# A row maximum on one core: 16 loads in place of 17, 56 blocks for GpSimd in place of 36, and results turned back four at a time

## The chip, the cores and the metric

The kernel runs on one core of one Trainium2 chip. The metric is the device time of one execution in microseconds (us); lower is better. A core has five engines that run side by side, each on its own queue of instructions: TensorE (PE), VectorE (DVE), ScalarE (ACT), GpSimd (POOL) and SyncE (SP). Transfers between the chip's main memory (HBM) and the core's on-chip memory (SBUF) run on 16 DMA engines; here SP issues the loads and ACT the stores. PSUM is the small memory that TensorE writes.

## The reference

The input is 64 MB of 4-byte numbers, and the output is the maximum of each row of 1024.

```python
def setup_inputs():
    batch, seq, dim = 32, 512, 1024
    return {"x": np.random.randn(batch, seq, dim).astype(np.float32)}

def reference(x):
    return np.max(x, axis=-1).astype(np.float32)
```

## The kernel before

The 16384 rows lie over 128 partitions, 128 rows to each. "A load of n rows" below means n rows of 1024 numbers on each partition, in one transfer. `BLOCKS` lists the loads in order: twelve of 2, 16, 14, 15, 13, 12, 10, 9, 8, 7, 6 and 4 rows, then five of 3, 2, 2, 1 and 1. The last 3 rows come in six column pieces, `PIECES`, of 640 to 384 columns, two pieces to a row; the second piece of a row has the first one's result in the cell ahead of it, so that its reduce covers both.

Loads land in a ring of `RING` = 47 rows. `issue` (L273) sends a load as soon as the program has named the last reader of the rows that it overwrites; SP then waits for these readers, and for an earlier transfer with the same semaphore, of which there are eight. The pieces (L278) follow the loads on the same queue.

`PLAN` is the order of all work, written out by hand; `in_turn` ties each engine to it. A step is a letter and a number:

- `d` and `p` are VectorE's reduces of load j (L76). `d` takes whole rows into the result tile `res`, and `p` takes the columns that VectorE keeps of the rows that it shares with GpSimd. `f` reduces a piece.
- `t`, `c`, `r`, `b`, `e` are GpSimd's share, by chunks of up to eight blocks of 128 columns. TensorE turns each 128x128 block into PSUM (`turn`, L155), so that a row of the input lies across the partitions. ACT copies the chunk to SBUF (`fetch`, L166). GpSimd takes the maximum over the partitions (`across`, L173), and all partitions then hold the results. TensorE turns them back from one row to a column, block by block (`back`, L184), and ACT copies the small columns out of PSUM (`keep`, L194).
- `m` is VectorE's merge of these with its own part: `m10` for load 10 and `m99` for all the last loads together, whose parts lie in `joint`.

`SHARED` says for each load how many rows are shared, how many blocks of each row go to GpSimd, and how many rows make a chunk:

```python
SHARED = {10: (6, 3, 2, 0), 12: (3, 3, 2, 0), 14: (2, 3, 1, 0), 16: (1, 3, 2, 0)}
```

That is 18 + 9 + 6 + 3 = 36 blocks in eight chunks. The functions `select` and `sums` stand in the code, and no step of the plan names them. Two stores end the kernel, both issued by ACT: the first behind the first piece's reduce (L313), the second behind everything on VectorE (L321).

Of the kernel before, what the change touches and what calls it, by code (L numbers as in the profile page):

```python
# [8 lines left out]
F32 = mybir.dt.float32  # L9
# [1 line left out]


BLOCKS = [
    [2, 16, 14, 15, 13, 12, 10, 9, 8, 7, 6, 4],
    [3, 2, 2, 1, 1],
]
RING = 47

SHARED = {10: (6, 3, 2, 0), 12: (3, 3, 2, 0), 14: (2, 3, 1, 0), 16: (1, 3, 2, 0)}


RANK = {12: 1, 14: 2, 16: 2}


PIECES = [(2, 640), (1, 512), (0, 576), (1, 512), (0, 448), (2, 384)]


PLAN = """  # L30
    d0 d1 d2 d3 d4 d5 d6 d7 d8 d9 t0 p10 t1 c0 r0 t2 c1 d11 r1 c2 b0 e0 r2 b1 e1 t3 p12 t4
    c3 b2 c4 r3 d13 e2 r4 m10 t5 p14 b3 c5 t6 r5 d15 e3 b4 c6 t7 p16 e4 r6 b5 f0 c7 e5 f1 r7
    b6 f2 e6 f3 b7 f4 e7 f5 m99
""".split()

NOSYNC = mybir.DependencyInfo(mybir.DependencyClass.NoSync, mybir.DependencyReason.DATA)
# [4 lines left out]
def kernel(  # L41
# [5 lines left out]
    nc = tc.nc  # L47
    P = 128
    X = mybir.AxisListType.X
    ALU = mybir.AluOpType  # L50

    xf = x.flatten_outer_dims()
    N, D = xf.shape
# [2 lines left out]
    of = out.flatten_outer_dims()  # L56

    once = ctx.enter_context(tc.tile_pool(name="once", bufs=1))
    turned = ctx.enter_context(tc.tile_pool(name="turned", bufs=2))
    allr = ctx.enter_context(tc.tile_pool(name="allr", bufs=2))  # L60
    psum = ctx.enter_context(tc.tile_pool(name="psum", bufs=2, space=bass.MemoryType.PSUM))
    psmall = ctx.enter_context(tc.tile_pool(name="psmall", bufs=4, space=bass.MemoryType.PSUM))

    ring = once.tile([P, I + RING * D], F32)
    res = ring[:, :I]
# [3 lines left out]
    def in_turn(engine, inst):  # L69
        if engine in latest:  # L70
            tc.add_manual_dep(inst.ins, latest[engine].ins.name, NOSYNC, reason="in turn")
        latest[engine] = inst
        return inst

    def maximum(out, in_):
        return in_turn("DVE", nc.vector.reduce_max(out=out, in_=in_, axis=X))  # L76

    ident = once.tile([P, P], F32)
    colno = once.tile([P, P], F32)
    rowno = once.tile([P, 32], F32)  # L80
    in_turn("DVE", nc.vector.memset(ident, 1.0))  # L81
    in_turn("DVE", nc.vector.memset(rowno, 0.0))
# [1 line left out]
        out=colno, data0=ident, data1=ident, initial=-1.0, op0=ALU.add, op1=ALU.mult))  # L84
    in_turn("DVE", nc.vector.transpose(out=rowno, in_=colno[:, :32]))  # L85
    for q in range(1, P // 32):
        part = rowno[q * 32:(q + 1) * 32, 0:1]
        in_turn("DVE", nc.vector.tensor_scalar(  # L88
            out=part, in0=part, scalar1=float(q * 32), scalar2=None, op0=ALU.add))
    in_turn("DVE", nc.vector.tensor_scalar(  # L90
        out=ident, in0=colno, scalar1=rowno[:, 0:1], scalar2=None, op0=ALU.is_equal))

    loads = []
    views = []
    last = 1 + max(r for r, _ in PIECES)
    first = at = 0
    for sizes in BLOCKS:
# [5 lines left out]
        base = len(loads)  # L103
        b, place = 0, {}
        for i in sorted(range(len(sizes)), key=lambda i: RANK.get(base + i, 0)):
            place[i] = b
            b += sizes[i]
        for i, n in enumerate(sizes):
            if at + n > RING:
                at = 0  # L110
            b = place[i]
# [3 lines left out]
    assert first == I  # L115
    shared = [SHARED.get(j, (0, C, 1, 0)) for j in range(len(loads))]

    lead = [n - s[0] for (_, n, _, _), s in zip(loads, shared)]
    final = [j for j in range(len(loads)) if j in RANK]
    final.sort(key=lambda j: loads[j][3])  # L120
# [2 lines left out]
    count = sum(shared[j][0] for j in final)  # L123
    width = max(shared[j][1] + (shared[j][1] < C) for j in final)
    joint = once.tile([P, count, width], F32)

    chunks = []
    for j, (m, parts, per, _) in enumerate(shared):
# [2 lines left out]
    def rows(j):  # L131
        start, n, _, _ = loads[j]
        return ring[:, I + start * D:I + (start + n) * D].rearrange("p (i d) -> p i d", d=D)

    filled, turns, tops = {}, {}, {}
    fetched = {}
    smalls = {}

    def share(j):
        m, parts, _, _ = shared[j]  # L140
        if j in RANK:
            r = loads[j][3] + lead[j] - col0
            return joint[:, r:r + m, :]
        if j not in fetched:
            fetched[j] = once.tile([P, m, parts + (parts < C)], F32, name=f"parts{j}")
        return fetched[j]

    def turn(k):
        j, r, q = chunks[k]
        parts = shared[j][1]  # L150
        ps = psum.tile([P, D], F32)
        for i in range(q):
            for c in range(parts):
                w = (i * parts + c) * P
                in_turn("PE", nc.tensor.transpose(  # L155
                    out=ps[:, w:w + P],
                    in_=rows(j)[:, lead[j] + r + i, c * P:(c + 1) * P],
                    identity=ident,
                ))
        filled[k] = ps  # L160

    def fetch(k):
        j, _, q = chunks[k]
        W = q * shared[j][1] * P
        sb = turned.tile([P, D], F32)
        in_turn("ACT", nc.scalar.copy(out=sb[:, :W], in_=filled[k][:, :W]))  # L166
        turns[k] = sb

    def across(k):
        j, _, q = chunks[k]  # L170
        W = q * shared[j][1] * P
        top = allr.tile([P, D], F32)
        in_turn("POOL", nc.gpsimd.partition_all_reduce(  # L173
            top[:, :W], turns[k][:, :W], P, bass_isa.ReduceOp.max))
        tops[k] = top

    def back(k):
        j, r, q = chunks[k]
        parts = shared[j][1]
        small = psmall.tile([P, q, parts], F32)  # L180
        for i in range(q):
            for c in range(parts):
                w = (i * parts + c) * P
                in_turn("PE", nc.tensor.transpose(  # L184
                    out=small[:, i, c:c + 1],
                    in_=tops[k][0:1, w:w + P],
                    identity=ident[0:1, 0:1],
                ))

        smalls[k] = small  # L190
# [2 lines left out]
        j, r, q = chunks[k]  # L193
        in_turn("ACT", nc.scalar.copy(out=share(j)[:, r:r + q, :shared[j][1]], in_=smalls[k]))  # L194

    def select(k):
        j, _, q = chunks[k]
        B = q * shared[j][1]
        view = tops[k][:, :B * P].rearrange("p (b w) -> p b w", w=P)
        in_turn("POOL", nc.gpsimd.affine_select(  # L200
            out=view, in_=view, pattern=[[0, B], [-1, P]], compare_op=ALU.is_equal,
            fill=0.0, base=0, channel_multiplier=1))

    def sums(k):
        j, r, q = chunks[k]
        parts = shared[j][1]
        for i in range(q):
            for c in range(parts):
                w = (i * parts + c) * P
                in_turn("ACT", nc.scalar.activation(  # L210
                    out=tops[k][:, w:w + P], in_=tops[k][:, w:w + P],
                    func=mybir.ActivationFunctionType.Copy,
                    accum_out=share(j)[:, r + i, c:c + 1]))

    def direct(j):
        _, n, _, col = loads[j]
# [4 lines left out]
    def partial(j):  # L221
        m, parts = shared[j][:2]

        s = width - parts if j in RANK else 1
        maximum(share(j)[:, :, parts:], rows(j)[:, lead[j]:lead[j] + m, parts * P:].rearrange(
# [15 lines left out]
    chained = {}  # L241
    for r, w in PIECES:
        c, q = done[r], before[r]
# [12 lines left out]
    readers = [0] * len(loads)  # L256
# [6 lines left out]
    behind = None  # L263
# [17 lines left out]
    taken = {}  # L281
    settled = -1
    gate = once.tile([P, 2], F32)
    steps = {"t": turn, "c": fetch, "r": across, "b": back, "e": keep, "s": select, "x": sums, "m": merge}
    for step in PLAN:
        issue()
        kind, k = step[0], int(step[1:])
# [8 lines left out]
        elif kind == "f":  # L296
            q = chained.get(k)
# [4 lines left out]
            inst = taken[k] = maximum(*tail[k])  # L302
            if q is not None:
                tc.declare_no_dep(inst.ins, taken[q].ins, reason="the wait stands ahead of it")
            if behind is None:
                behind = inst
# [44 lines left out]
```

## Time and profile before

| what | value |
|---|---|
| median of 3 runs | 163.49 us (163.42 to 163.67) |
| the profiled execution | 163.5 us |
| its span in the profile | 161.7 us |
| VectorE busy | 135.5 us (84%), 33 instructions |
| GpSimd busy | 15.9 us (10%), 8 all-reduces |
| PE, ACT busy | 13.2 us, 7.3 us |
| HBM read | 67.11 MB, mean 415 GB/s over the span |

The span runs from the first instruction to the last that the profiler saw; the execution's time has 1.8 us around it. In the page's slices the span is cut into 40 equal parts, and each digit is the busy share of a part in tenths. A group's row gives the line, the engine and the operation, output from input with their shapes, the count, the busy time in us, the mean ns of one, and the idle time before it with what ended it. In the timeline, rows that follow each other are merged, with their count behind an x. In the chain of work that ended last, "issue" is time in which the engine waited for nothing that the profile shows, and SPq and DVEq are the sequencers of these engines.

### The profile page before, as it was taken

How to read it: one execution, taken by the hardware profiler on the slowest of the kernel's cores; microseconds unless marked ns; L12 is line 12 of the kernel's file. 1: busy time of each engine (PE TensorE's matmuls, PEld its weight loads, DVE VectorE, ACT ScalarE, POOL GpSimd, SP SyncE). 2: the span in 40 equal slices, each digit the busy share in tenths (PEclk: the TensorE clock that was granted, in tenths of full speed). 3: DMA queues.
4: the chain of work that ended last, by engine and by line, in shares of the span. 5: the costliest groups of instructions: out<-in, count | busy, mean ns of one | idle time of the engine just before them, and what ended most of it. 6: DMA issues, size and time to landing. Idle time of an engine off the chain costs nothing.

```text
span 161.7 us, 306 instructions
## 1 busy us (share of the span) xinstructions
PE 13.2 (8%) x72; PEld 11.1 (7%) x72; DVE 135.5 (84%) x33; ACT 7.3 (5%) x17; POOL 15.9 (10%) x13
## 2 busy tenths in 40 slices
PE   0000000000000000000000000000000000647481
PEld 0000000000000000000000000000000000636350
DVE  3500008999999929999999999999999999999994
ACT  0020000000000000000000000000000000142230
POOL 0000000000000000000000000000000000098991
PEclk9999999999999999999999999999999999995555
DMA  5997997899999699999988998999999899999991
GB/s 192 586 470 308 519 458 326 383 454 454 486 486 456 274 454 421 421 435 550 425 389 389 486 456 355 438 438 421 430 478 426 369 478 413 401 431 422 398 388 51
DMA packets 3600, 67.18 MB, mean 415 GB/s; under 512 B 656, under 2 KB 912, under 8 KB 1680
## 3 DMA queue, kind: packets, MB, share of 16 engines
q1 hardware_dynamic: 3312, 67.11, 97.0%
q10 hardware_dynamic: 288, 0.07, 0.2%
HBM read 67.11 MB, written 0.07 MB: 415 GB/s over the span
## 4 chain that ended last, share of the span: by engine, by line
DMA 62%; DVE 35%; SPq 0%; issue 0%; DVEq 0%
DMA ring<-in_x_dram 62%; DVE ring L76 35%; SPq L273 0%; DVEq L346 0%
## 5 line engine op out<-in xcount | busy, mean ns | idle before, releaser
L76 DVE TENSOR_REDUCE ring<-ring 128x2 f32<-128x2048 f32 (+17 forms) x19 | 125.7, 6661 | 23.1 <-DMA ring<-in_x_dram 23.0
L173 POOL PARTITION_ALL_REDUCE top<-sb x8 | 15.6, 2011 | 134.9 <-ACT sb L166 134.5
L155 PE MATMUL ps<-ident,ring 128*128 128x128 f32 x36 | 8.8, 419 | 141.2 <-DMA ring<-in_x_dram 141.0
L155 PEld LDWEIGHTS ps<-ident,ring 128*128 128x128 f32 x36 | 7.0, 221 | 141.3 <-issue 141.3
L166 ACT COPY sb<-ps 128x768 f32<-128x768 f32 (+1 forms) x8 | 5.0, 640 | 139.1 <-PE ps L155 137.7
L184 PE MATMUL small<-ident,top 1*128 1x1 f32 x36 | 4.8, 238 | 4.5 <-POOL top L173 4.5
L184 PEld LDWEIGHTS small<-ident,top 1*128 1x128 f32 x36 | 4.1, 197 | 6.4 <-POOL top L173 5.0
L76 DVE TENSOR_REDUCE joint<-ring 128x3 f32<-128x1920 f32 (+2 forms) x3 | 4.4, 1483 | 0.0
L76 DVE TENSOR_REDUCE parts<-ring 128x6 f32<-128x3840 f32 x1 | 4.2, 4150 | 0.0
L166 ACT ACT_TABLE_LOAD x1 | 1.3, 1283 | 7.8 <-DVE ring L76 7.8
L194 ACT COPY joint<-small 128x3 f32<-128x3 f32 (+1 forms) x5 | 0.8, 164 | 2.3 <-PE small L184 2.3
L81 DVE MEMSET ident<- 128x128 f32 x1 | 0.2, 165 | 0.8 <-PEq L335 0.8
L293 POOL MEMSET gate<- 128x1 f32 x1 | 0.1, 98 | 7.3 <-DVE ring L76 7.3
L194 ACT COPY parts<-small 128x6 f32<-128x6 f32 x3 | 0.5, 165 | 2.6 <-PE small L184 2.5
L88 DVE TENSOR_SCALAR rowno<-rowno 32x1 f32<-32x1 f32 x3 | 0.4, 146 | 0.1
L83 DVE TENSOR_TENSOR_SCAN colno<-ident 128x128 f32<-128x128 f32 x1 | 0.4, 424 | 0.0
L90 DVE TENSOR_SCALAR ident<-colno,rowno 128x128 f32<-128x128 f32 x1 | 0.3, 285 | 0.0
L85 DVE STREAM_TRANSPOSE rowno<-colno 128x32 f32<-128x32 f32 x1 | 0.2, 211 | 0.0
L76 DVE TENSOR_REDUCE ring<-parts 128x6 f32<-128x24 f32 x1 | 0.2, 171 | 0.0
L76 DVE TENSOR_REDUCE ring<-joint 128x6 f32<-128x24 f32 x1 | 0.2, 171 | 0.0
L335 POOL MEMSET const-float32-0.0<- 128x1 f32 x1 | 0.1, 98 | 0.2 <-issue 0.2
L335 POOL MEMSET const-bfloat16-1.0<- 128x1 bf16 x1 | 0.1, 101 | 0.0
(3 smaller groups left out, 0.3 us busy)
## 6 DMA issues: line engine op xcount, KB each, us to landing
ring<-in_x_dram SPq DMA_DIRECT2D x1, 7680.0 KB, 57.8
ring<-in_x_dram SPq DMA_DIRECT2D x1, 7168.0 KB, 40.1
ring<-in_x_dram SPq DMA_DIRECT2D x1, 6656.0 KB, 33.6
ring<-in_x_dram SPq DMA_DIRECT2D x1, 6144.0 KB, 33.1
ring<-in_x_dram SPq DMA_DIRECT2D x1, 5120.0 KB, 26.2
ring<-in_x_dram SPq DMA_DIRECT2D x1, 4608.0 KB, 36.7
ring<-in_x_dram SPq DMA_DIRECT2D x1, 4096.0 KB, 32.9
ring<-in_x_dram SPq DMA_DIRECT2D x1, 3584.0 KB, 28.3
```

What stands on the lines that cost most here:

```text
L76: return in_turn("DVE", nc.vector.reduce_max(out=out, in_=in_, axis=X))
L81: in_turn("DVE", nc.vector.memset(ident, 1.0))
L83: in_turn("DVE", nc.vector.tensor_tensor_scan(out=colno, data0=ident, data1=ident, initial=-1.0, op0=ALU.add, op1=ALU.mult))
L85: in_turn("DVE", nc.vector.transpose(out=rowno, in_=colno[:, :32]))
L88: in_turn("DVE", nc.vector.tensor_scalar(out=part, in0=part, scalar1=float(q * 32), scalar2=None, op0=ALU.add))
L90: in_turn("DVE", nc.vector.tensor_scalar(out=ident, in0=colno, scalar1=rowno[:, 0:1], scalar2=None, op0=ALU.is_equal))
L155: in_turn("PE", nc.tensor.transpose(out=ps[:, w:w + P], in_=rows(j)[:, lead[j] + r + i, c * P:(c + 1) * P], identity=ident,))
L166: in_turn("ACT", nc.scalar.copy(out=sb[:, :W], in_=filled[k][:, :W]))
L173: in_turn("POOL", nc.gpsimd.partition_all_reduce(top[:, :W], turns[k][:, :W], P, bass_isa.ReduceOp.max))
L184: in_turn("PE", nc.tensor.transpose(out=small[:, i, c:c + 1], in_=tops[k][0:1, w:w + P], identity=ident[0:1, 0:1],))
L194: in_turn("ACT", nc.scalar.copy(out=share(j)[:, r:r + q, :shared[j][1]], in_=smalls[k]))
L335: nc = _bacc.Bacc("TRN2", target_bir_lowering=False, num_devices=1)
```

## The change

The load list has eleven loads in the first block in place of twelve: 2, 16, 16, 13, 15, 13, 12, 10, 9, 6, 4. The pieces get other sizes, and the last has 480 columns. GpSimd takes 56 blocks of loads 7 to 15, in twelve chunks. The merges are `m7` to `m10` and `m99`, and `m99` stands ahead of the last piece's reduce.

The fourth number of a `SHARED` entry now chooses how a chunk is turned back. With a 1 there, a new step `g` (`gather`) puts a tile `four` together: since all partitions hold the same results, ACT copies block 4g + a from the partitions 32a to 32a + 31 to the same partitions of `four`, for a = 0 to 3, one copy for each a. TensorE then turns each 128x128 group of `four` back in one transpose (`together`), and `keep` picks every 32nd column. With a 0, blocks are turned back singly, as before.

The buffers for `turn`, `fetch`, `across` and the results in PSUM are fixed tiles used in rotation, and the waits of a writer for the earlier writer of the same tile are declared away, since it is behind that tile's readers. `select` and `sums` are gone.

```diff
 BLOCKS = [
-    [2, 16, 14, 15, 13, 12, 10, 9, 8, 7, 6, 4],
+    [2, 16, 16, 13, 15, 13, 12, 10, 9, 6, 4],
     [3, 2, 2, 1, 1],
 ]
-SHARED = {10: (6, 3, 2, 0), 12: (3, 3, 2, 0), 14: (2, 3, 1, 0), 16: (1, 3, 2, 0)}
-RANK = {12: 1, 14: 2, 16: 2}
-PIECES = [(2, 640), (1, 512), (0, 576), (1, 512), (0, 448), (2, 384)]
+SHARED = {7: (3, 2, 4, 1), 8: (2, 8, 1, 1), 9: (2, 7, 1, 1), 10: (4, 1, 8, 1), 11: (2, 2, 2, 1), 12: (2, 2, 4, 0), 13: (2, 2, 1, 0), 14: (1, 2, 2, 1), 15: (1, 2, 4, 0)}
+RANK = {11: 1, 12: 2, 13: 2, 14: 2, 15: 2}
+PIECES = [(1, 608), (2, 576), (0, 544), (1, 416), (2, 448), (0, 480)]
 PLAN = """
-    d0 d1 d2 d3 d4 d5 d6 d7 d8 d9 t0 p10 t1 c0 r0 t2 c1 d11 r1 c2 b0 e0 r2 b1 e1 t3 p12 t4
-    c3 b2 c4 r3 d13 e2 r4 m10 t5 p14 b3 c5 t6 r5 d15 e3 b4 c6 t7 p16 e4 r6 b5 f0 c7 e5 f1 r7
-    b6 f2 e6 f3 b7 f4 e7 f5 m99
+    d0 d1 d2 d3 d4 d5 d6 t0 d7 c0 r0 g0 b0 e0 p7 m7 d8 t1 t2 c1 r1 c2 r2 g1 t3 d9 b1 c3 t4
+    e1 r3 g2 c4 b2 p9 p10 t5 e2 r4 g3 c5 b3 e3 r5 t6 g4 m8 d11 p11 c6 b4 g5 r6 t7 p12 e4 b5
+    c7 e5 r7 g6 m9 m10 p13 t8 t9 c8 b6 r8 c9 b7 e6 p14 t10 e7 r9 c10 b8 p15 t11 e8 r10 c11
+    f0 b9 e9 f1 r11 g10 f2 b10 f3 b11 e10 f4 e11 m99 f5
 """.split()
...
+    fours = ctx.enter_context(tc.tile_pool(name="fours", bufs=2))
...
+    psums = [psum.tile([P, D], F32, name=f"psum{i}") for i in range(2)]
+    backs = psum.tile([P, 4, D // 2], F32)
+    turned = [once.tile([P, D], F32, name=f"turned{i}") for i in range(2)]
+    allr = [once.tile([P, D], F32, name=f"allr{i}") for i in range(2)]
...
     def back(k):
         j, r, q = chunks[k]
         parts = shared[j][1]
-        small = psmall.tile([P, q, parts], F32)
+        if shared[j][3]:
+            together(k)
+            return
+        small = results(k)[:, :q * parts].rearrange("p (i c) -> p i c", i=q)
...
+    def gather(k):
+        j, _, q = chunks[k]
+        B = q * shared[j][1]
+        four = fours.tile([P, D // P // 4, P], F32)
+        view = tops[k].rearrange("p (g a w) -> p g a w", a=4, w=P)
+        for a in range(min(4, B)):
+            part = slice(32 * a, 32 * (a + 1))
+            n = (B - a + 3) // 4
+            in_turn("ACT", nc.scalar.copy(out=four[part, :n, :], in_=view[part, :n, a, :]))
+        fourth[k] = four
+
+    def together(k):
+        j, _, q = chunks[k]
+        B = q * shared[j][1]
+        small = results(k)
+        for g in range((B + 3) // 4):
+            n = 32 * min(4, B - 4 * g)
+            backwards(k, nc.tensor.transpose(
+                out=small[:, g * P:g * P + n], in_=fourth[k][:n, g, :], identity=ident[:n, :n]))
+        smalls[k] = small.rearrange("p (b w) -> p b w", w=32)[:, :B, 0:1].rearrange(
+            "p (i c) w -> p i (c w)", i=q)
```

More of the change, by code (lines that the diff above doesn't have):

```diff
@@ L58 @@
     once = ctx.enter_context(tc.tile_pool(name="once", bufs=1))
[L59 to L62, printed above, removed]
+    fours = ctx.enter_context(tc.tile_pool(name="fours", bufs=2))
+    psum = ctx.enter_context(tc.tile_pool(name="psum", bufs=1, space=bass.MemoryType.PSUM))
     ring = once.tile([P, I + RING * D], F32)
@@ L78 @@
     ident = once.tile([P, P], F32)
-    colno = once.tile([P, P], F32)
+    four = fours.tile([P, D // P // 4, P], F32)
+    colno = four[:, 0, :]
     rowno = once.tile([P, 32], F32)
@@ L136 @@
     fetched = {}
-    smalls = {}
+    smalls, fourth = {}, {}
+    turners, fetchers, acrossed, turnbacks = {}, {}, {}, {}
     def share(j):
@@ L146, in share, with renewed @@
         return fetched[j]
+    def renewed(inst, writers, k):
+        for i in range(k % 2, k, 2):
+            for old in writers[i]:
+                tc.declare_no_dep(inst.ins, old.ins, reason="behind its readers")
     def turn(k):
@@ L150, in turn @@
         parts = shared[j][1]
-        ps = psum.tile([P, D], F32)
+        ps = psums[k % 2]
+        turners[k] = []
         for i in range(q):
@@ L154, in turn @@
                 w = (i * parts + c) * P
-                in_turn("PE", nc.tensor.transpose(
+                inst = in_turn("PE", nc.tensor.transpose(
                     out=ps[:, w:w + P],
@@ L159, in turn @@
                 ))
+                renewed(inst, turners, k)
+                turners[k].append(inst)
         filled[k] = ps
@@ L164, in fetch @@
         W = q * shared[j][1] * P
-        sb = turned.tile([P, D], F32)
-        in_turn("ACT", nc.scalar.copy(out=sb[:, :W], in_=filled[k][:, :W]))
+        sb = turned[k % 2]
+        inst = in_turn("ACT", nc.scalar.copy(out=sb[:, :W], in_=filled[k][:, :W]))
+        renewed(inst, fetchers, k)
+        fetchers[k] = [inst]
         turns[k] = sb
@@ L171, in across, with results, backwards @@
         W = q * shared[j][1] * P
-        top = allr.tile([P, D], F32)
-        in_turn("POOL", nc.gpsimd.partition_all_reduce(
+        top = allr[k % 2]
+        inst = in_turn("POOL", nc.gpsimd.partition_all_reduce(
             top[:, :W], turns[k][:, :W], P, bass_isa.ReduceOp.max))
+        renewed(inst, acrossed, k)
+        acrossed[k] = [inst]
         tops[k] = top
+    def results(k):
+        return backs[:, k % 4, k // 4 % 2 * 256:(k // 4 % 2 + 1) * 256]
+    def backwards(k, inst):
+        in_turn("PE", inst)
+        for i in range(k % 8, k, 8):
+            for old in turnbacks[i]:
+                tc.declare_no_dep(inst.ins, old.ins, reason="behind its readers")
+        turnbacks.setdefault(k, []).append(inst)
     def back(k):
@@ L183, in back @@
                 w = (i * parts + c) * P
-                in_turn("PE", nc.tensor.transpose(
+                backwards(k, nc.tensor.transpose(
                     out=small[:, i, c:c + 1],
@@ L194, in keep @@
         in_turn("ACT", nc.scalar.copy(out=share(j)[:, r:r + q, :shared[j][1]], in_=smalls[k]))
-    def select(k):
+    def gather(k):
         j, _, q = chunks[k]
         B = q * shared[j][1]
[L199 to L213, printed above, removed]
+        four = fours.tile([P, D // P // 4, P], F32)
+        view = tops[k].rearrange("p (g a w) -> p g a w", a=4, w=P)
[10 more added lines that the diff above has]
+            n = 32 * min(4, B - 4 * g)
+            backwards(k, nc.tensor.transpose(
+                out=small[:, g * P:g * P + n], in_=fourth[k][:n, g, :], identity=ident[:n, :n]))
+        smalls[k] = small.rearrange("p (b w) -> p b w", w=32)[:, :B, 0:1].rearrange(
+            "p (i c) w -> p i (c w)", i=q)
     def direct(j):
@@ L283 @@
     gate = once.tile([P, 2], F32)
-    steps = {"t": turn, "c": fetch, "r": across, "b": back, "e": keep, "s": select, "x": sums, "m": merge}
+    steps = {"t": turn, "c": fetch, "r": across, "b": back, "e": keep, "g": gather, "m": merge}
     for step in PLAN:
```

## The prediction, made before the changed kernel was run

> **What bounds the kernel now.** I read the page's slices and queue rows first, to see which engine is full.
>
> ```profile
> DVE  3500008999999929999999999999999999999994
> POOL 0000000000000000000000000000000000098991
> DMA  5997997899999699999988998999999899999991
> q1 hardware_dynamic: 3312, 67.11, 97.0%
> ```
>
> VectorE is full from the middle on, but so are the DMA engines from the first slice to the last but one. Loads fill 97.0% of 16 engines' span. What is left, 3.0% of 161.7 = 4.9 us, is nearly all outside the stream: 1.1 us before it and 3.4 us after the last landings. Next, the table by stretches (stretch and its length, then PE, PEld, DVE, ACT, POOL, clock, DMA share, GB/s), to see whether the stream slows when its loads shrink.
>
> ```profile
> 2.00:24.00 22.00, 0.00 (x0) 0.00 (x0) 2.74 (x4) 1.28 (x1) 0.10 (x1) 1.00 1.00 427
> 114.00:138.00 24.00, 0.00 (x0) 0.00 (x0) 24.00 (x3) 0.00 (x0) 0.00 (x0) 1.00 0.98 423
> 150.00:158.00 8.00, 4.77 (x27) 3.53 (x26) 7.97 (x10) 2.18 (x9) 7.62 (x5) 0.50 1.02 394
> ```
>
> The DMA share is about 1 everywhere; the rate falls only from 427 to 394 GB/s in the stretch with some nine small loads. Last, the chain that ended last (start us, us, what).
>
> ```profile
> 90.09 0.02 issue
> 90.12 23.69 DVE ring L76 x2
> 113.81 0.02 issue
> 113.82 0.33 SPq L273
> ...
> 149.74 8.58 DMA ring<-in_x_dram
> 158.32 0.02 issue
> 158.34 0.50 DVE ring L76
> 158.85 0.04 issue
> 158.88 0.55 DVE ring L76
> 159.43 0.09 DVEq L346
> ```
>
> The fifth piece's reduce starts 0.02 us after the piece lands at 158.32, and the sixth 0.54 later. So VectorE has no backlog at the end: it works in step with the landings, and the store follows. The end is the end of the stream plus one reduce and one store. The chain's stretch on VectorE at 90.12 frees the ring for loads that start many microseconds later; the DMA share shows no hole there.
>
> **The change, part by part.** The profiled execution took 163.5 us, 1.8 more than its span; the median shown is 163.49. I sum against 163.5.
>
> *The stream.* The bytes are the same; there are 22 transfers in place of 23. What one costs: in 150 to 158 the rate is 394 against 427, so 8 x (1 - 394/427) = 0.62 us is lost over some nine transfers, 0.07 each. One less: -0.07 us. Alone it cannot give more than the idle time inside the stream and these 0.07 allow, about 0.5 us.
>
> Every load must still be issued in time. Landings follow from 1.21 us a row (90.09 - 24.72 over 54 rows) and 1.22 later (149.72 - 90.09 over 49). VectorE's reduces follow 0.15 us + 1.042 ns an element (17.22 for 16384, 0.82 for 640), each starting up to 0.09 before the last one's end. The fifth load (15 rows) waits for the reduce of the first 16, over at 41.9; the stream needs it at 58.8. The later ones come to 61.3 for 77.0, 75.2 for 92.7, 94.1 for 107.2, 108.0 for 119.3, 121.1 for 142.4. The pieces wait for the transfer eight (the last: seven) before them on their semaphore: the last is issued at 153.3 and needed at 157.1, a cover of 3.8 us. The first load, 2 rows, took 4.7 us from issue to landing, so issue and completion cost about 2.3 of those; all covers exceed it. No hole: 0.
>
> One rule speaks against the new sizes. The Trainium skill (DMA: Bandwidth & Descriptors, How a descriptor splits into AXI transactions) says a transfer that doesn't start on a 256-byte boundary fetches from the boundary below and pays for the unused bytes. The pieces of 416 and 480 columns now start 128 bytes past one (608 x 4 = 9.5 x 256; 544 x 4 = 8.5 x 256); all six of before start on one, so no run here shows the price. By the rule: an estimate of 2 pieces x 128 partitions x 128 bytes at 427 GB/s = 0.08 us, which would bring the sum to +0.02.
>
> *The tail.* The last piece grows from 384 to 480 columns: 96 x 1.042 ns = +0.10 us on the last reduce. The joint merge (m99) moves ahead of it; behind it, it cost 159.51 - 159.42 = 0.09: -0.09. Now it fits between the fifth piece's reduce, which ends about when the last piece lands (0.65 us apart for 480 columns, 0.62 + 0.09 of work), for about +0.02. The first store is issued on ACT behind the last keep, before the last reduce ends: 0.
>
> *VectorE.* 20 more blocks of 128 columns leave it: 2560 x 1.042 ns = -2.7 us; it gets 30 reduces of L76 in place of 25, at 0.06 of overhead: +0.3. The rest is idle time, as the loads come no sooner. But four merges (m7 to m10) and m99 now wait in VectorE's queue for ACT's keeps, with the next reduces queued behind them, and the landings leave little room. Walking it through: d8 at 131.2 (landed 131.2), p10 143.4, p13 152.05 (landed 152.0), f0 155.5, f4 158.06 (landed 158.04), f5 158.71. So what holds it over about 0.5 us before p13, or at m99, costs about one for one, less some 0.4 us of idle between p13 and f5.
>
> *GpSimd.* Three all-reduces of 768 columns in a row took 7.47 us and three of 384 took 4.23, so they start 2.49 and 1.41 apart: 0.33 us + 2.81 ns a column.
>
> ```profile
> 141.35 7.47 POOL L173 PARTITION_ALL_REDUCE top<-sb  x3 [133.48 <-ACT sb L166]
> 154.12 4.23 POOL L173 PARTITION_ALL_REDUCE top<-sb  x3 [0.38 <-PE small L184]
> ```
>
> That makes 512 columns 1.77 (between the rows), 896 2.85, 1024 3.21 and 256 1.05 (outside). Total: 2.49 + 2 x 3.21 + 2 x 2.85 + 3 x 1.77 + 4 x 1.05 = 24.1 us against 15.6, over 35 us in place of 17. Bounds: 256 between 0.94 (in proportion to 384) and 1.41 (no cheaper than 384); 1024 between 3.2 and 3.8 (in proportion to 384). I take the line, nearest 768 and 384.
>
> *ACT's gathers.* 30 copies of 32 partitions, 128 or 256 columns, out of SBUF; the trace has only copies out of PSUM at 128 partitions.
>
> ```profile
> L166 ACT COPY sb<-ps 128x768 f32<-128x768 f32 x4 | 3.2, 799 | 134.8 <-PE ps L155 133.4 <-POOL top L173 1.3
> L166 ACT COPY sb<-ps 128x384 f32<-128x384 f32 x4 | 1.9, 481 | 4.3 <-PE ps L155 4.3
> L194 ACT COPY joint<-small 128x3 f32<-128x3 f32 x4 | 0.7, 164 | 2.1 <-PE small L184 2.1
> ```
>
> The line through these, 0.16 us + 0.83 ns a column, gives 0.27 and 0.37. Ends: 0.16 (as small as the keep) and 0.80 (as the 768 copy). I take the line: a quarter of the partitions should cost no more. A gather of eight blocks is then 1.2 us, of four 0.8. I walked the whole plan through: at 0.48 a copy the end moves by 0.1; at 0.60 the merges would come late and the end by 1.9 us.
>
> *TensorE.* 36 transposes to one column (0.11 apart at the granted clock of 0.50) become 13 wide ones (0.21 apart, as L155's 18 in 3.92) and 10 narrow; 56 forward ones in place of 36. All beside the stream; it never fills.
>
> *The two narrow places.* m10 waits for chunk 5, turned back behind the forward transposes of chunk 7, whose load lands at 149.6: four transposes to 150.7, the turn back to 151.1, keep to 151.4; VectorE comes to m10 at 151.8. m99 waits for chunk 11: chunk 7's fetch ends at 151.3, its all-reduce starts at 151.4, then 1.77 + 3 x 1.05 + 1.14 to 157.5, the turns back and keeps to 158.2; VectorE comes to it at 158.6. The same walk over the kernel before puts its last all-reduce 0.2 us too early, so I count 0.2 us of slack at m99. Cost: 0.
>
> Sum: -0.07 + 0.10 - 0.09 + 0.02 = -0.04, so 163.46; with that much uncertainty 163.4.
>
> **The rivals.** *The GpSimd chain ends late (slower).* From 151.4 on, five all-reduces run without a gap and m99 stands ahead of the last reduce. It decides from 0.2 us of lateness. For it: narrow slack, four sizes outside the rows. Against: 384 and 512 are inside, and 768 and 384 fit the kernel before to 0.2 us. If 256 columns cost 1.41, three starts and the last one's length add 1.44, less 0.2 to 0.4: about +1.1, 164.6; half of that gives 164.0.
>
> *ACT's copies are dear (slower).* At 0.60 each, late gathers hold fetches in ACT's queue and so GpSimd: +1.9, 165.4. For: an operand not seen here. Against: every ACT row lies on one line.
>
> *VectorE was the bound (faster).* If the 0.50 us on VectorE at 158.34 were backlog, 2.4 us less work would take it away: 163.0. Against: that reduce starts 0.02 us after its landing.
>
> *Each transfer has a large price (faster).* The first load took 4.7 us from issue to landing, and 2 rows are 2.4 us of bytes: 2.3 fixed. If that showed in full for each transfer, one less would give 161.2. Against: 23 of them would be 53 us, but 67.11 MB at 427 GB/s is 157.2 us, which fills the stretch from 1.13 to 158.3. The Trainium skill (DMA: Bandwidth & Descriptors, its fit of a DMA's time to its bytes, taken with software descriptors) has 2.0 us a DMA; here the trace disagrees, since transfers overlap.
>
> **How the numbers follow.** 0.2%, 0.33 us, is about what a measurement of this kernel can tell from no change. Forecast within that: 0.61. GpSimd's chain late 0.17, dear copies 0.06, an unforeseen hold of a merge on VectorE 0.04: slower 0.27. VectorE as the bound 0.10, transfer price 0.02: faster 0.12. The range runs from 163.1, which takes in part of the third rival, to 164.4, just under the upper bound for 256 columns; it leaves out dear copies, the transfer price and the ends.
>
> **What would show it.** Right: DMA share still about 1 to 157.9, last landing within 0.1 us of before, f5 starting at its landing, m99 with no wait. Wrong: VectorE waiting for ACT ahead of m10 or m99; all-reduces of 256 columns over 1.25 us apart; gather copies over 0.5 us; a hole in the DMA row; f5 starting before 158.5.

## The result, and the profile after

| | before | changed |
|---|---|---|
| median, 6 runs each | 163.51 us (163.42 to 163.67) | 164.74 us (164.65 to 165.00) |
| profiled execution, its span | 163.5 us, 161.7 us | 164.8 us, 163.0 us |

The changed kernel is slower: ratio 1.0076, 95% interval 1.0063 to 1.0089. The forecast was no change at 163.4 us, with a range up to 164.4; the time lies above it. The span grew by 1.3 us.

First the slices and the queues, as before. The page of the changed kernel:

```profile
DVE  3500009999499999994899999999999999999991
POOL 0000000000000000000000000000006009898960
DMA  5996995995999999999999989989989999999970
q1 hardware_dynamic: 3168, 67.11, 96.1%
q14 instruction: 1, 0.01, 0.0%
```

The loads fill the DMA engines as before. The row of `q14` is new: one packet of 0.01 MB of kind "instruction" inside the span. The experiments below tie such packets to the length of an engine's program. By the packets' records it has 8192 bytes and runs from 159.20 to 159.65.

The table by stretches, in the prediction's columns:

```profile
2.00:24.00 22.00, 0.00 (x0) 0.00 (x0) 2.74 (x4) 1.28 (x1) 0.10 (x1) 1.00 1.02 433
114.00:138.00 24.00, 5.96 (x24) 4.78 (x24) 23.89 (x5) 4.60 (x9) 5.98 (x3) 1.00 0.97 419
150.00:158.00 8.00, 5.74 (x25) 3.71 (x24) 7.91 (x11) 5.33 (x21) 7.33 (x6) 1.00 1.00 392
```

The rates are those of before within 2%, and the last load packet ends at 158.26, against 158.33 before. So the loads did not slow.

The end is in the timeline (start us, us, engine, line, operation, output from input; ACTq rows are DMA issues on ACT's queue). In the kernel before, the two stores and VectorE's last reduce were these:

```profile
158.98 0.37 ACTq L313 DMA_DIRECT2D out_dram<-ring  x1
159.34 0.17 DVE L76 TENSOR_REDUCE ring<-joint 128x6 f32<-128x24 f32 x1
159.54 0.34 ACTq L321 DMA_DIRECT2D out_dram<-ring  x1
```

In the changed kernel, ACT's rows first and then VectorE's:

```profile
158.16 0.16 ACT L225 COPY joint<-backs 128x2 f32<-128x2 f32 x1 [0.25 <-PE backs L215]
158.53 2.16 ACTq L348 DMA_DIRECT2D out_dram<-ring  x1
160.79 0.39 ACTq L356 DMA_DIRECT2D out_dram<-ring  x1
158.72 0.17 DVE L75 TENSOR_REDUCE ring<-joint 128x8 f32<-128x24 f32 x1
158.81 0.64 DVE L75 TENSOR_REDUCE ring<-ring 128x1 f32<-128x481 f32 x1
```

VectorE is done at 159.45, against 159.51 before. But the first store took 2.16 us to issue (0.37 before) and held ACT's queue until 160.70. The second store, ready at 159.45, was issued at 160.79 in place of 159.54. That 1.25 us is the whole loss (the medians differ by 1.23), and the instruction packet lies inside the slow issue.

### The profile page after: what moved, and what is told of

Its sections match the earlier page's. It is cut to its first block, busy times and chain, and to the rows that moved or that the text cites. A ratio compares the mean times of both kernels' runs of the same rounds, so it can differ in the third digit from the quotient of the medians.

```text
span 163.0 us, 367 instructions
## 1 busy us (share of the span) xinstructions
PE 19.6 (12%) x79; PEld 14.4 (9%) x79; DVE 133.2 (82%) x38; ACT 21.1 (13%) x55; POOL 24.5 (15%) x17
## 2 busy tenths in 40 slices
DMA packets 3457, 67.18 MB, mean 412 GB/s; under 512 B 640, under 2 KB 1024, under 8 KB 1664
## 4 chain that ended last, share of the span: by engine, by line
DMA 64%; DVE 31%; SPq 1%; issue 1%; DVEq 0%
DMA ring<-in_x_dram 64%; DVE ring L75 29%; DVE joint L75 2%; SPq L308 1%; DVEq L381 0%
## 5 line engine op out<-in xcount | busy, mean ns | idle before, releaser
L75 DVE TENSOR_REDUCE ring<-ring 128x16 f32<-128x16384 f32 (+13 forms) x17 | 118.1, 6984 | 25.1 <-DMA ring<-in_x_dram 25.1
L189 POOL PARTITION_ALL_REDUCE allr<-turned x12 | 24.2, 2061 | 125.6 <-ACT turned L180 125.2
L167 PE MATMUL psum<-ident,ring 128*128 128x128 f32 x56 | 14.4, 428 | 129.7 <-DMA ring<-in_x_dram 129.7
L180 ACT COPY turned<-psum 128x256 f32<-128x256 f32 (+4 forms) x12 | 7.9, 657 | 121.7 <-PE psum L167 121.4
L167 PEld LDWEIGHTS psum<-ident,ring 128*128 128x128 f32 x56 | 10.8, 222 | 131.3 <-issue 124.7
L236 ACT COPY four<-allr 32x256 f32<-32x256 f32 (+1 forms) x30 | 10.6, 352 | 5.7 <-POOL allr L189 5.4
L75 DVE TENSOR_REDUCE joint<-ring 128x2 f32<-128x1536 f32 (+1 forms) x5 | 6.9, 1427 | 0.1
L75 DVE TENSOR_REDUCE parts<-ring 128x3 f32<-128x2304 f32 (+2 forms) x3 | 6.7, 2278 | 0.0
L245 PE MATMUL backs<-ident,four 128*128 128x128 f32 (+2 forms) x13 | 4.6, 425 | 8.8 <-ACT four L236 8.8
L245 PEld LDWEIGHTS backs<-ident,four 128*128 128x128 f32 (+2 forms) x13 | 2.3, 202 | 11.1 <-ACT four L236 10.5
```

Of the source, the lines that this page charges most:

```text
L167: inst = in_turn("PE", nc.tensor.transpose(out=ps[:, w:w + P], in_=rows(j)[:, lead[j] + r + i, c * P:(c + 1) * P], identity=ident,))
L180: inst = in_turn("ACT", nc.scalar.copy(out=sb[:, :W], in_=filled[k][:, :W]))
L189: inst = in_turn("POOL", nc.gpsimd.partition_all_reduce(top[:, :W], turns[k][:, :W], P, bass_isa.ReduceOp.max))
L236: in_turn("ACT", nc.scalar.copy(out=four[part, :n, :], in_=view[part, :n, a, :]))
L245: backwards(k, nc.tensor.transpose(out=small[:, g * P:g * P + n], in_=fourth[k][:n, g, :], identity=ident[:n, :n]))
```

## The experiments

Theory A: ACT's program has grown by 36 instructions (the trace has 34 rows of ACT before and 70 after), and at about its 65th ACT has to wait until a further piece of its instructions is fetched. The slow store is the 64th of ACT's rows in the trace; the expectations count it as the program's 65th instruction. Rival B: the slow store comes from what the new plan does around it. The kernel before was run again with each group; its medians there were 163.73 to 163.77 us, 0.2 us above the 163.51 of the result, so ratios are against the runs of the same group.

**36 more ACT instructions in the kernel before.** They are copies of one column, from 9 us on, in ACT's idle time.

```diff
+                for _ in range(36):
+                    in_turn("ACT", nc.scalar.copy(out=gate[:, 0:1], in_=ident[:, 0:1]))
```

> The kernel before, with 36 tiny ACT copies (128x1) put in ACT's queue at 9 us, where ACT idles until 139; its first store is then the 65th ACT instruction of the program, as in the changed kernel. Theory A (ACT runs out of fetched instructions there, and the store waits some 1.8 us for the 8192-byte instruction transfer): the first store's issue takes about 2.2 us in place of 0.37, an instruction packet of 0.01 MB appears among the queues, 164.7 us. Rival B (the store is slow through what the changed plan does around it on VectorE, ACT and the DMA rings): issue 0.37 us, no packet, 163.5 us.

Measured 165.88 us, ratio 1.0131 (1.0117 to 1.0145). The queue row, and the timeline of ACT's end in this kernel:

```profile
q14 instruction: 1, 0.01, 0.0%
159.57 2.15 ACTq L315 DMA_DIRECT2D out_dram<-ring  x1
161.82 0.39 ACTq L323 DMA_DIRECT2D out_dram<-ring  x1
```

The kernel before, with not a load, block or transpose changed, shows the same 2.15 us and the same packet. Theory A holds so far and B falls. The loss was 2.1 us, more than the 1.2 foreseen: its store starts later (159.57 for 158.53), because the last keep here ends at 159.36.

**The same padding in the changed kernel, 56 copies.** The place then falls long before the end.

> The changed kernel with 56 tiny ACT copies at 9 us, where ACT idles until 122: the 65th ACT instruction is then in chunk 0's gather, some 30 us ahead of the end and with 3 us of slack before m7. Theory A: the instruction transfer moves to about 126 us, the first store's issue takes 0.4 us, last reduce still over at about 159.45, 163.4 us. Rival B: no change, 164.7 us.

Measured 164.09 us, ratio 1.0019 (1.0010 to 1.0028). Most of the loss was undone, not all. ACT's timeline at the end, then a row of VectorE:

```profile
158.96 0.38 ACTq L350 DMA_DIRECT2D out_dram<-ring  x1
160.23 0.34 ACTq L358 DMA_DIRECT2D out_dram<-ring  x1
25.76 17.22 DVE L75 TENSOR_REDUCE ring<-ring 128x16 f32<-128x16384 f32 x1 [17.85 <-DMA ring<-in_x_dram]
```

The stores are quick again. But the packet now runs at 24.53, not at 126: it came while ACT stood at its first `fetch` step, the 61st of its rows, a few instructions ahead of the place. There it met the load stream, and the reduce of the first 16 rows started at 25.76, against 24.83 in the changed kernel. Of the 16 completions of that load, fifteen came by 24.97 and one at 25.74. So one DMA engine had been held up, and one completion of each later load stayed late: the last load packet ended at 158.97, against 158.26.

**Stores from SP.** Both kernels, with the two stores on SP's queue, ahead of its last wait:

```diff
-        store = nc.scalar.dma_start(out=dst, in_=src)
+        store = nc.sync.dma_start(out=dst, in_=src)
...
+    nc.sync.dma_start(out=views[-1][0], in_=views[-1][1])
     seen = nc.sync.nop(nofuse=True)
...
-    nc.scalar.dma_start(out=views[-1][0], in_=views[-1][1])
```

> The changed kernel with both stores issued by SP in place of ACT. Theory A: the stores are issued at about 158.3 and 159.5 in 0.4 us each, and what ACT waits for lies behind its last keep, beside the store: 163.4 us. Rival B: if the store is slow through the DMA rings or the waits on VectorE, it is as slow from SP: 164.7 us.

> The kernel before with both stores issued by SP in place of ACT. Both theories: 163.4 to 163.5 us, since its stores took 0.37 and 0.34 us to issue; it is there so that the changed kernel with stores from SP has its own yardstick.

Measured 163.52 us for the changed kernel, ratio 0.9988 (0.9979 to 0.9997), and 163.70 us for the kernel before, ratio 0.9998 (0.9989 to 1.0007). SP's rows in the timeline of the changed kernel with SP's stores, and VectorE's last:

```profile
156.62 0.35 SPq L348 DMA_DIRECT2D out_dram<-ring  x1
159.57 0.34 SPq L353 DMA_DIRECT2D out_dram<-ring  x1
158.90 0.64 DVE L75 TENSOR_REDUCE ring<-ring 128x1 f32<-128x481 f32 x1
```

ACT still fetches its packet, at 159.75, but that is behind the last load packet (158.39), and no store waits for ACT. This version is faster than the kernel before (163.73 in the same group), by 0.2 us, and 1.2 us under the changed kernel's 164.74. Without the fetch in its way, the change is worth about -0.2 us.

**Fewer ACT instructions.** The chunks of loads 14 (two copies fewer) or 11 and 14 (six fewer) are turned back singly: the fourth number of their `SHARED` entries is 0, and their `g` steps are gone.

> The changed kernel, with chunk 10 alone turned back singly, so that ACT has two copies fewer: its first store is the 63rd ACT instruction, its second the 65th. Theory A1 (a fixed place in ACT's instructions, about the 65th, is where it waits for the transfer): the first store's issue takes 0.4 us, the wait moves to the second store, instruction packet still there, 164.5 to 165.0 us. Rival A2 (whatever the place, the first store on ACT triggers the instruction transfer when ACT's program is long): first store 2.2 us again, 164.7 us. Rival A3 (the gather of chunk 10 just ahead of the store is the cause): 163.5 us, no packet.

> The changed kernel, with chunks 6 and 10 turned back singly: the first store is the 60th ACT instruction, the second the 62nd. Theory A1: both stores issue in 0.4 us; the transfer, if it comes, comes behind them, 163.4 to 163.6 us. Rival A2: 164.7 us.

Measured 163.70 us, ratio 0.9997 (0.9988 to 1.0006), and 163.76 us, ratio 1.0002 (0.9993 to 1.0011). ACT's end with two copies fewer:

```profile
158.44 0.37 ACTq L348 DMA_DIRECT2D out_dram<-ring  x1
159.70 0.34 ACTq L356 DMA_DIRECT2D out_dram<-ring  x1
```

Two ACT copies fewer, and nearly all of the loss is gone. That denies A2: the packet is still there, at 160.03, and the first store is quick. A3 expected no packet, and the kernel before with padding has the slow store without any gather, so A3 falls too. But my A1 had the second store wait, as the 65th instruction, and 164.5 us or more; it did not, though it is now the 64th of ACT's rows. So the count tells about where the packet comes, and not which instruction's record carries the wait; why a first store at that place took 2.16 us and a second one 0.34 stays open. With six copies fewer the packet comes at 162.34, behind the end of the span (162.0).

Both medians stay 0.2 us over the 163.52 with SP's stores, and the profiles show where: from the second store's issue to the end of the span it takes 2.34 and 2.39 us here, and 2.17 to 2.23 in the ten other profiles. With two copies fewer the store lands 1.58 us after its issue, in place of 1.41 to 1.47, with the packet beside it.

**No gathers at all.** All twelve chunks are turned back singly, with ACT's stores and with SP's.

> The changed kernel without the gathers: all twelve chunks turned back block by block, the rest as changed (16 loads, 56 blocks). ACT has 30 copies fewer, TensorE 46 narrow transposes in place of 13 wide ones. Theory A1: no instruction packet, stores issue in 0.4 us, 163.4 us, the loss undone without touching loads or blocks. Rival C (the loss is in the loads and blocks and only shows at the store): 164.7 us. Were the gathers needed to keep m10 or m99 in time, VectorE would wait for ACT there and the last reduce would end after 159.5.

> The same without gathers, with both stores issued by SP. By theory A1 the same as with ACT's stores to within 0.1 us, 163.3 to 163.5 us; it tells whether the transfer that ACT still fetched behind its last keep in the run with gathers and SP's stores cost anything there (that run: 163.52 us).

Measured 164.88 us, ratio 1.0065 (1.0052 to 1.0077), and 164.92 us, ratio 1.0069 (1.0055 to 1.0082). A1's number was a clear miss, though ACT's packet is gone and the stores are quick (0.37 and 0.34 us). VectorE's last rows without gathers (ACT's stores), and a queue row:

```profile
156.00 1.44 DVE L75 TENSOR_REDUCE ring<-ring 128x1 f32<-128x608 f32 x2
158.43 1.74 DVE L75 TENSOR_REDUCE ring<-ring 128x1 f32<-128x544 f32 x3 [0.99 <-DMA ring<-in_x_dram]
160.17 0.64 DVE L75 TENSOR_REDUCE ring<-ring 128x1 f32<-128x481 f32 x1
q8 instruction: 1, 0.02, 0.0%
```

VectorE stood 0.99 us for the third piece, and the loads' last packet ended at 159.66 in place of 158.26. `q8` has another instruction packet, of 16384 bytes, from 156.22 to 157.32. The trace has 132 rows of TensorE besides its matmuls, in place of 92, so it looked like TensorE's own fetch, with one of the 16 DMA engines held for 1.1 us (theory D). The completions fit: fifteen of the third piece's 16 came by 157.27, and one at 158.40. Rival C, that the loss is in the loads and blocks, has the time right, but the runs with SP's stores and with fewer ACT copies have these loads and blocks without the loss. Rival E was that single turns are too slow. Two runs tell D and E apart.

> The changed kernel with gathers for the eight- and seven-block chunks 1 to 4 alone; the other chunks are turned back singly. TensorE has some 45 instructions fewer than without gathers, ACT 14 fewer than with all. Theory D (the run without gathers lost its 1.2 us to TensorE's own instruction transfer of 16384 bytes, which held one of the 16 DMA engines for 1.1 us at 156.2 and so every piece behind it): no instruction packet ahead of the last landing, stores issued in 0.4 us, 163.5 to 163.7 us. Rival E (turning back singly is too slow for the landings, and the packet is beside the point): the small chunks, which end the stream, are all turned back singly here, so 164.5 us or more.

> The changed kernel with the stores from SP, which took 163.52 us, and 60 more transposes on TensorE at 8 us, where it idles until 120. Theory D (an instruction transfer is paid by the load stream, since each load needs all 16 DMA engines): a 16384-byte instruction packet at about 147 us; the landings behind it come 1.0 to 1.3 us later, and so does the end: 164.5 to 164.8 us. Rival E: the added transposes lie in idle time and change nothing: 163.5 us.

With gathers for chunks 1 to 4 alone, the end inside the span is as in the kernels without a fetch: span 161.8, second store at 159.67, the small chunks turned back singly without a late reduce. E falls. The execution took 163.77 to 165.30 us, median 164.61, ratio 1.0042 (1.0024 to 1.0060), over my 163.7. The loss lies outside the span: some executions were about 1 us longer than others, with spans of 161.8 to 162.2. In the one that was profiled, of 164.93 us, packets of 16384 and 8192 bytes came at 163.70 and 163.84, behind the span's end. That these made it longer is not shown: no short execution was profiled.

With 60 transposes more on TensorE and SP's stores: 164.72 us, ratio 1.0061 (1.0046 to 1.0075), as theory D has it, 1.2 us over the version with SP's stores alone. The edit and a row of VectorE's timeline:

```diff
+                for _ in range(60):
+                    in_turn("PE", nc.tensor.transpose(out=psums[1][:, :P], in_=ident, identity=ident))
```

```profile
144.98 3.89 DVE L75 TENSOR_REDUCE parts<-ring 128x4 f32<-128x3584 f32 x1 [1.02 <-DMA ring<-in_x_dram]
```

The 16384-byte packet, foreseen at about 147, runs at 142.80 for 1.07 us. Of the 16 completions of the load then on its way, fifteen came by 143.80 and one at 144.96. The lateness lasts to the end (last load packet at 159.43, against 158.39), though these transposes were done in TensorE's idle time. The granted clock of TensorE was lower in these runs (0.54 to 0.57, against 0.93 to 1.00 with SP's stores alone), but this load had been issued at 121.56, and a slower TensorE would not leave one completion of 16 late. E falls here too.

## Why the prediction was wrong

**The step that failed** is one sentence of the tail: "The first store is issued on ACT behind the last keep, before the last reduce ends: 0." Issue before the reduce ends it was, at 158.53 against 159.45. But the 0 holds only if the issue is as short as the 0.37 us of before. It took 2.16, and the second store, which the sum let follow VectorE at once, stands behind it on ACT: +1.25 us that the sum put at nothing. I costed what each new ACT instruction takes on the engine, and not what the number of them does to the engine's instruction supply. None of my rivals had this mechanism; the trace of before has such packets of 8192 bytes on `q14` only ahead of the span. That the time lies near the 164.6 of the rival with a late GpSimd chain is chance: that chain was in time.

The Trainium skill (Runtime: NRT & Kernel Launch, Instruction fetch mechanics) says that an engine's instructions come in 16 KiB blocks of 256, fetched ahead over the engine's own DMA queue, with the cost of a crossing mostly hidden. The traces agree that fetches run over DMA queues, and on 16384 bytes for TensorE. They disagree on the rest: ACT's packet has 8192 bytes and comes at about its 65th program instruction; the store issued there took 1.8 us longer, so the fetch was not hidden; and with TensorE's packet the loads ended 1.0 to 1.4 us later.

**The steps that held:**

- *Stream, -0.07.* The last load packet ended at 158.26, against 158.33. With SP's stores it was 158.39 against 158.53. Single profiles of the same loads differ by 0.2, so the size is not settled.
- *VectorE's walk.* f4 at 158.20 (walked 158.06), f5 at 158.81 (158.71), over at 159.45. The walk's 158.71 would end at 159.36, 0.15 under the 159.51 of before, which does not fit the sum's -0.04; the sum was the nearer. VectorE's waits name DMA alone, and no merge waited for ACT.
- *GpSimd.* The five all-reduces from 151.64 took 6.06 us; the prediction had 151.4 to 157.5, the same length 0.2 earlier. The line for 256 columns was right.
- *The narrow places.* m99's keep ended at 158.32 and VectorE came at 158.72: a slack of 0.4, where I counted 0.2.
- *Unaligned pieces.* Packets of 1664 and 1920 bytes, which start 128 past a boundary, took 69 and 80 ns (medians). The aligned ones of the same run, 74 for 1792 bytes and 98 for 2432, put 69 and 79 on their line. So the 0.08 us that the prediction estimated by the rule of the Trainium skill (DMA: Bandwidth & Descriptors, How a descriptor splits into AXI transactions) is not seen. With it the sum would have been +0.04, not the +0.02 that the prediction states.

```profile
151.64 6.06 POOL L189 PARTITION_ALL_REDUCE allr<-turned  x5 [0.29 <-ACT parts L225]
L236 ACT COPY four<-allr 32x256 f32<-32x256 f32 x16 | 6.4, 403 | 5.1 <-POOL allr L189 5.0
L236 ACT COPY four<-allr 32x128 f32<-32x128 f32 x14 | 4.1, 295 | 0.6 <-POOL allr L189 0.5
```

*ACT's gathers* were mis-sized without harm: 0.40 and 0.30 us a copy, not 0.37 and 0.27, and they do not overlap, as the prediction's 1.2 us for a gather of eight blocks needs (4 x 0.37 is 1.5); it took 1.65. ACT's idle time took that up.

The sum without the store, -0.04 us, is what the version with SP's stores can be held against: its median lies 0.18 under that of the kernel before with the same stores, and in the two profiles 0.14 of it is in the stream. The forecast of no change was right to within 0.2 us for the work, and wrong for the program that carries it.

## What to carry to other kernels

Count instructions for each engine, not only their durations. An engine that runs past what was fetched of its program can hold up a store that stands there, and the packet itself holds one DMA engine: in the four runs where it fell inside the load stream, the loads ended 0.7 to 1.4 us later. Look in the queue rows for packets of kind "instruction" inside the span, and at DMA issues that take over 2 us where others take 0.4. Put the last store on an engine with a short program, as SP here, or keep the program of the engine that issues it below the place. Where ACT's packet fell behind the last landing, it cost nothing to be seen with SP's stores, and by the profiles about 0.2 us with two and six copies fewer.

## What the runs showed of the hardware that was not expected

- ACT fetched 8192 bytes in each run with 59 or more rows of ACT in the trace, and in none with 46 or fewer. In two runs the first store was ACT's 64th row and took 2.15 to 2.16 us in place of 0.37; where the second store was the 64th row, it took 0.34.
- TensorE's packet has 16384 bytes and took 1.07 to 1.10 us amid loads, in three runs. The load then on its way was complete only when its last of 16 completions came, 1.1 to 1.3 us behind the other fifteen.
- ACT's 8192 bytes in the load stream cost 0.7 us, though the packet took 0.31: one completion of 16 came 0.77 after the others.
- With both packets behind the end of the span (16384 bytes at 163.70), some executions were about 1 us longer than others at equal spans; that the packets are the cause is not shown.
